# Weights packed in reading order, a transposed copy of x, packed bias columns and a four-block first stream in a hybrid encoder layer

## The chip, the core and the metric

The kernel runs on one core of a Trainium2 chip. The metric is device time in microseconds, the median of three runs: 1731.29 us before the change (1729.61 to 1732.01). The names of the engines are those of the profile: PE multiplies matrices (PEld is its weight load), DVE, ACT and POOL work elementwise, SP issues the DMAs.

## The reference

One layer of a hybrid encoder, for 256 tokens of 2048 channels, in float32:

```
proj   = x @ w_in + b_in                      # [256, 15384]
y_a    = forgetting_attention(q, k, v, log_sigmoid(f))          # 8 heads of 128
y_b    = u * (masked w_s @ group_layer_norm(v) + b_s)           # spatial gating, 8 groups
y_c    = gated_delta_rule(silu(conv4(qkv)), decays, betas)      # 8 heads, chunks
merged = sum_i sigmoid(gate_i) * (y_i @ w_proj_i)               # 3 x [1024, 2048]
x1     = layer_norm(2**0.25 * x + merged @ w_out)
h      = conv3(x1 @ w_up) + conv_b                              # [2048, 11008]
out    = layer_norm(2**0.25 * x1 + (silu(h_gate) * h_val) @ w_down)   # [5504, 2048]
```

The weights are 80 million float32 numbers and are each used once.

## The kernel before

Every large product is a **weight stream**. The helper `wload` (L117 to L125) brings 512 KB of weights into one of four `raw` buffers with one DMA on SP's queue (L122), and `split` (L113 to L115) makes two float32r parts of it: ACT copies the high part into `wh` (L114), DVE subtracts to get the low part `wl` (L115). There are four `wh` and four `wl` buffers. The activations are split in the same way, so a product is a sum of high by high, low by high and high by low.

`stream_b` (L162 to L184) computes two blocks of 128 channels for all 256 tokens: for each of 16 blocks of 128 input channels and for each of its two output blocks there is one matmul with 512 columns (L178: the high weights by x's high and low parts side by side) and one with 256 columns (L179: the low weights by the high part). In the text such two matmuls are called a pair; a stream has 32 pairs, and four 512 KB tiles feed it. `stream_a` (L127 to L160) computes 512 channels for the two token blocks with three matmuls of 512 columns each (L134 to L136).

The DeltaNet projections come first, as twelve streams of the kind `stream_b` (L814 to L840): four of keys, four of queries, four of values. Within the first, `load_x` (L249 to L254) loads x with the tokens on the partitions, transposes it on PE (L243) and splits it into `xhl`. After each stream comes an epilogue with a causal conv (L826 to L834), most of it on DVE. The projections of attention and spatial gating, the gates, the three branch projections, `w_out`, and the feed-forward part follow.

The smaller work of the mixers is written as Python generators in a list `queue`. After each of the 16 blocks of a stream `tick` runs the oldest generator to its next `yield`, so that this work lies between matmuls of the stream. `small_columns` (the gates' 24 columns, L280 to L377) and `gdn_decays` enter the list after the first stream, `gdn_keys` after the four key streams. `gdn_keys` multiplies key products into the decays `am` (DVE, L432), scales `am` (POOL, L443, by the factors `fa` of L439), sends its diagonal blocks through DRAM (L451, L454), inverts them by an elimination of 31 steps on POOL (L462, L464) and writes the result `td` (L467). `gdn_inverse`, put into the list after the last value stream, reads it into `T` (L482), transposes it on DVE (L488) and goes on on PE (L502).

A scheduler with a timeline model orders the instructions of each engine at build time; on the chip each engine follows its list strictly in order. SP too: a DMA that waits holds up every DMA behind it.

Columns of biases and conv weights are loaded as rows of 128 and transposed on PE by `rows_to_cols` (L224 to L232; the transpose is L229), ten uses' worth of columns in eight transposes. The mixing matrices of the spatial gating are transposed on PE as well (L775).

Of the kernel before, what the change touches and what calls it, by code (L numbers as in the profile page):

```python
# [10 lines left out]
F32 = mybir.dt.float32  # L11
# [8 lines left out]
P = 128  # L20
# [22 lines left out]

@with_exitstack
def trunk_kernel(ctx, tc, x, w_in, b_in, sgu_ln_g, sgu_ln_b, sgu_w, sgu_b, gdn_conv_w, gdn_a_log,
                 gdn_dt_bias, gdn_norm_g, w_proj_a, w_proj_b, w_proj_c, w_out, ln1_g, ln1_b,
                 ffn_w_up, ffn_conv_w, ffn_conv_b, ffn_w_down, ln2_g, ln2_b, out):
    nc = tc.nc
    x, w_in, sgu_w, gdn_conv_w = x[0], w_in[0], sgu_w[0], gdn_conv_w[0]
    w_proj = [w_proj_a[0], w_proj_b[0], w_proj_c[0]]  # L50
    w_out, ffn_w_up, ffn_conv_w, ffn_w_down = w_out[0], ffn_w_up[0], ffn_conv_w[0], ffn_w_down[0]
    out = out[0]

# [63 lines left out]
    def wload(src, k0, nk, c0, n, dst=None, low=nc.vector, ahead=150):  # L117
        """Weight rows k0*128.. (nk blocks), columns c0..c0+n: list over blocks of (high, low) views."""
        with tc.high_priority(offset=ahead):
            raw = wraw.tile([P, 1024], F32, tag="raw", name=nm("raw"))  # L120
            rv = raw[:, 0:nk * n].rearrange("p (k n) -> p k n", n=n)
# [6 lines left out]
    def stream_a(src, nkb, c0, lh, ll, k_off=0, tail=0, spare=(), spare_last=False, done=None, pre=None):  # L128
        """[tokens, 512] outputs for both token blocks; the last tail k blocks go block by block of tokens."""
# [9 lines left out]
        for k0 in range(0, head, 2):  # L139
            nk = min(2, head - k0)  # L140
            ws = wload(src, k_off + k0, nk, c0, 512)
# [8 lines left out]
        for i, k0 in enumerate(starts):  # L150
            j = i - (len(starts) - len(spare)) if spare_last else (i if i < len(spare) else -1)
            ws += wload(src, k_off + k0, min(2, nkb - k0), c0, 512, spare[j] if j >= 0 else None,
# [9 lines left out]
    def stream_b(src, c0, n, act, pre=None):  # L162
        """n//128 blocks of [128 channels, (main 256 | low part 256)]."""
        nb = n // P
        accs = [acc() for _ in range(nb)]
        nk = 1024 // n
        for k0 in range(0, KB, nk):
            if pre is not None:
                pre(k0)
            ws = wload(src, k0, nk, c0, n, ahead=150 if pre is None else 1)  # L170
            for j in range(nk):
                kb = k0 + j
                wh, wl = ws[j]
                for i in range(nb):
                    a = accs[i]
                    cs = slice(i * P, (i + 1) * P)
                    if kb < KB - 1:
                        nc.tensor.matmul(a, wh[:, cs], act[:, kb, :], start=kb == 0, stop=False)  # L178
                        nc.tensor.matmul(a[:, 0:S], wl[:, cs], act[:, kb, 0:S], start=False, stop=False)  # L179
                    else:  # L180
                        nc.tensor.matmul(a[:, 0:S], wl[:, cs], act[:, kb, 0:S], start=False, stop=False)  # L181
                        nc.tensor.matmul(a, wh[:, cs], act[:, kb, :], start=False, stop=True)  # L182
                tick()
        return accs  # L184

    def stream_b_halves(src, c0, act):
        """As stream_b for 2 blocks, the tokens block by block: [128 channels, (main 2 x 128 | low part 2 x 128)]."""
        accs = [acc() for _ in range(2)]
        ws = []
        for k0 in range(0, KB, 4):  # L190
            ws += wload(src, k0, 4, c0, 256, low=nc.gpsimd)
# [14 lines left out]
    def rsqrt(dst, src, n):  # L206
        """dst = src ** -0.5 for positive normal src, by Newton steps."""
# [7 lines left out]
    def rsqrt_column(dst, src):  # L215
        """The same for one column; the steps y <- y (y^2 src - 3) leave powers of two to the end."""
# [7 lines left out]
    def rows_to_cols(src_rows, nr, name):  # L224
        """DRAM rows [nr, 128] -> SBUF [128, nr]."""
        r = wk.tile([P, 512], F32, tag="wk", name=nm("rows"))
        nc.sync.dma_start(r[0:nr, 0:P], src_rows)
        p = mx()
        nc.tensor.transpose(p[:, 0:nr], r[0:nr, 0:P], ident[0:nr, 0:nr])  # L229
        c = const.tile([P, nr], F32, name=name)  # L230
        nc.vector.tensor_copy(c, p[:, 0:nr])
        return c  # L232

# [13 lines left out]
    x_sb = resp.tile([P, 2, D], F32, tag="res", name="x_sb")  # L247
# [76 lines left out]
        # softplus(z) = max(z, 0) + log1p(exp(-|z|)); z = -f for the forget gates, a + dt for the decays  # L324
# [12 lines left out]
        # log1p(e) = 2 atanh(e / (2 + e))  # L337
# [20 lines left out]
        # rows [16, 256] (forget: whole sequence; decay: per 128 tokens)  # L358
# [21 lines left out]
    def inv_norm(ss, name):  # L380
        """1 / norm [128 tokens, 2, 8] from sums of squares [128, 16]."""
# [750 lines left out]
```

## Time and profile before

| | us |
|---|---|
| median of three runs | 1731.29 |
| lowest and highest | 1729.61, 1732.01 |
| span of the profiled execution, first to last instruction | 1727.9 |
| PE busy | 1689.7 (98%) |
| DVE, ACT, POOL busy | 1119.2, 780.9, 262.5 |
| HBM read | 321.38 MB, 188 GB/s over the span |
| DMA engines, mean busy share | 63.0% for the queue of the program's DMAs |

The page gives the span of the profiled execution and no separate time for it; the median of the timed runs is 3.4 us above that span. PE is busy in nearly every slice of the span. What it leaves idle, some 38 us, lies in four places: the first ten microseconds, the stretch from 80 to 190 us, the first layer norm near 980 us, and the last layer norm after 1712 us.

### The profile page before, as it was taken

The page shows a single profiled execution, that of the slowest core. Times are in us where ns is not written, and L with a number is a line of the kernel's source. Part 1 is how long each engine was busy: PE and PEld are TensorE (multiplying, and loading weights), DVE is VectorE, ACT ScalarE, POOL GpSimd, SP SyncE. Part 2 cuts the span into 40 slices and gives each one's busy share as a digit, 9 for nine tenths or more (in the row PEclk, how much of TensorE's full clock was granted, in tenths as well). Part 3 has the DMA queues.
Part 4 walks back from the last instruction along what each step waited for, and adds up shares of the span by engine and source line. Part 5 has one row for each costly group of instructions (what it writes and reads, how often), then busy time and mean ns, then how long its engine had stood idle before and what let it go on. Part 6 is the DMA issues. An engine that isn't in the chain of part 4 may idle for free.

```text
span 1727.9 us, 22873 instructions
## 1 busy us (share of the span) xinstructions
PE 1689.7 (98%) x8738; PEld 1435.5 (83%) x8738; DVE 1119.2 (65%) x1516; ACT 780.9 (45%) x985; POOL 262.5 (15%) x213
## 2 busy tenths in 40 slices
PE   8989999999999999999999999999999999999996
PEld 7877898888888888888888788888888888888885
DVE  5999555577665555555555777775567776567767
ACT  5543444354444444444443355544344544344542
POOL 0259030304230000100100301110001110001102
PEclk9999899999999999999999999999999999999998
DMA  8563646766666666666676476666666665666653
GB/s 239 171 183 97 172 113 196 240 182 173 194 191 206 200 201 206 199 198 200 198 268 213 148 219 183 184 185 195 192 190 185 184 188 191 194 185 194 185 178 112
DMA packets 245249, 325.51 MB, mean 188 GB/s; under 512 B 18844, under 2 KB 159764, under 8 KB 244116
## 3 DMA queue, kind: packets, MB, share of 16 engines
q1 hardware_dynamic: 245140, 324.06, 63.0%
q8 instruction: 68, 1.11, 0.3%
q14 instruction: 41, 0.34, 0.1%
HBM read 321.38 MB, written 2.64 MB: 188 GB/s over the span
## 4 chain that ended last, share of the span: by engine, by line
PE 91%; DVE 6%; issue 1%; DMA 1%; ACT 0%; DVEq 0%; SPq 0%; ACTq 0%
PE acc L178 24%; PE acc L136 16%; PE acc L134 16%; PE acc L135 16%; PE acc L179 12%; PE acc L182 2%; DVE wl L115 1%; DVE cv L832 1%; PE acc L181 1%; DVE z L974 1%; PE mx L243 1%; DVE cv L830 0%; DVE z L973 0%; ACT wh L114 0%; DMA x_sb<-in_x_dram 0%
## 5 line engine op out<-in xcount | busy, mean ns | idle before, releaser
L115 DVE TENSOR_TENSOR wl<-raw,wh 128x1024 fp32r<-128x1024 f32 (+1 forms) x568 | 716.7, 1263 | 494.7 <-ACT wh L114 485.8
L114 ACT ACTIVATE wh<-raw 128x1024 fp32r<-128x1024 f32 x572 | 603.8, 1056 | 686.4 <-PE acc L136 417.2
L178 PE MATMUL acc<-x1hl,wh 128*128 128x512 f32 x1260 | 446.6, 398 | 0.0
L179 PE MATMUL acc<-x1hl,wl 128*128 128x256 f32 x1260 | 354.0, 281 | 0.0
L178 PEld LDWEIGHTS acc<-x1hl,wh 128*128 128x128 f32 x1260 | 236.7, 188 | 56.4
L178 PE MATMUL acc<-xhl,wh 128*128 128x512 f32 x720 | 259.6, 402 | 2.4 <-ACT wh L114 2.4
L179 PEld LDWEIGHTS acc<-x1hl,wl 128*128 128x128 f32 x1260 | 238.1, 189 | 1.7
L134 PE MATMUL acc<-wh,xhl 128*128 128x512 f32 x576 | 226.6, 393 | 0.0
L135 PE MATMUL acc<-wl,xhl 128*128 128x512 f32 x576 | 224.5, 390 | 0.0
L136 PE MATMUL acc<-wh,xhl 128*128 128x512 f32 x576 | 224.4, 390 | 0.0
L179 PE MATMUL acc<-xhl,wl 128*128 128x256 f32 x720 | 205.8, 286 | 7.2 <-DVE wl L115 7.2
L178 PEld LDWEIGHTS acc<-xhl,wh 128*128 128x128 f32 x720 | 137.0, 191 | 33.0 <-ACT wh L114 2.7
L1076 POOL TENSOR_TENSOR cvv<-cvv,cvg 128x256 f32<-128x256 f32 x43 | 56.5, 1332 | 607.3 <-DVE cvv L1047 607.3
L179 PEld LDWEIGHTS acc<-xhl,wl 128*128 128x128 f32 x720 | 137.9, 192 | 11.8 <-DVE wl L115 10.5
L136 PE MATMUL acc<-wh,aL 128*128 128x512 f32 x328 | 127.6, 389 | 0.0
L135 PE MATMUL acc<-wl,aH 128*128 128x512 f32 x328 | 127.6, 389 | 0.0
L134 PE MATMUL acc<-wh,aH 128*128 128x512 f32 x328 | 127.6, 389 | 0.0
L136 PEld LDWEIGHTS acc<-wh,xhl 128*128 128x128 f32 x576 | 108.1, 188 | 22.5
L135 PEld LDWEIGHTS acc<-wl,xhl 128*128 128x128 f32 x576 | 108.2, 188 | 21.9
L134 PEld LDWEIGHTS acc<-wh,xhl 128*128 128x128 f32 x576 | 108.2, 188 | 21.9
L945 POOL TENSOR_TENSOR merged<-merged,wk 128x512 f32<-128x512 f32 x16 | 28.3, 1787 | 362.9 <-DVE wk L943 362.9
L135 PEld LDWEIGHTS acc<-wl,aH 128*128 128x128 f32 x328 | 61.6, 188 | 12.9
(352 smaller groups left out, 1898.3 us busy)
## 6 DMA issues: line engine op xcount, KB each, us to landing
raw<-in_w_in_dram SPq DMA_DIRECT2D x240, 512.0 KB, 3.7
raw<-in_ffn_w_up_dram SPq DMA_DIRECT2D x172, 512.0 KB, 3.9
raw<-in_ffn_w_down_dram SPq DMA_DIRECT2D x84, 512.0 KB, 4.3
raw<-in_w_out_dram SPq DMA_DIRECT2D x32, 512.0 KB, 4.4
raw<-in_w_proj_a_dram SPq DMA_DIRECT2D x16, 512.0 KB, 3.6
raw<-in_w_proj_b_dram SPq DMA_DIRECT2D x16, 512.0 KB, 3.6
raw<-in_w_proj_c_dram SPq DMA_DIRECT2D x16, 512.0 KB, 3.7
wk<-in_b_in_dram SPq DMA_DIRECT2D x18, 256.0 KB, 3.9
```

The source lines that it names most:

```text
L114: nc.scalar.activation(dst_h, src, AF.Copy)
L115: low.tensor_sub(dst_l, src, dst_h.bitcast(F32))
L134: nc.tensor.matmul(a, lh(kb, tb), w[0], start=kb == 0, stop=False)
L135: nc.tensor.matmul(a, lh(kb, tb), w[1], start=False, stop=False)
L136: nc.tensor.matmul(a, ll(kb, tb), w[0], start=False, stop=kb == nkb - 1)
L178: nc.tensor.matmul(a, wh[:, cs], act[:, kb, :], start=kb == 0, stop=False)
L179: nc.tensor.matmul(a[:, 0:S], wl[:, cs], act[:, kb, 0:S], start=False, stop=False)
L181: nc.tensor.matmul(a[:, 0:S], wl[:, cs], act[:, kb, 0:S], start=False, stop=False)
L182: nc.tensor.matmul(a, wh[:, cs], act[:, kb, :], start=False, stop=True)
L243: nc.tensor.transpose(pv[:, i, tb * P:(tb + 1) * P], src(kb, tb), ident)
L945: nc.gpsimd.tensor_add(merged[:, tb, cs], merged[:, tb, cs], gts[tb])
L1076: nc.gpsimd.tensor_mul(cv, cv, cvg[i])
```

## The change

All arrays are now prepared on the host before the launch in the order in which the kernel reads them, and the kernel reads them by new addresses. The part of the diff that does this on the host is not shown in full; its core is `pack`, which lays each 256- or 512-column piece of a weight matrix out as [128 partitions, blocks of 128 rows, columns]. A 512 KB tile is then 4 KB in one run on each partition, where it was four runs of 1 KB or two of 2 KB.

```
+    def tiles(src, nkb, n, first=0):
+        def at(t, k0, nk):
+            return bass.AP(tensor=src.tensor, offset=src.offset + first + t * nkb * P * n + k0 * n,
+                           ap=[[nkb * n, P], [1, nk * n]])
+        return at
...
-            nc.sync.dma_start(rv, src[k0 * P:(k0 + nk) * P, c0:c0 + n].rearrange("(k p) n -> p k n", p=P))
+            nc.sync.dma_start(raw[:, 0:nk * n], src(k0, nk))
...
-    def stream_b(src, c0, n, act, pre=None):
+    def stream_b(srcs, n, act, steps=None, pre=None, more=()):
...
-        accs = [acc() for _ in range(nb)]
+        accs = list(more) + [acc() for _ in range(nb * len(srcs) - len(more))]
...
+        for nk in steps or [nk] * (KB // nk):
...
+            ws = [wload(src, k0, nk, n, ahead=150 if pre is None else 1) for src in srcs]
...
-    def load_x(kb):
-        for tb in range(2):
-            nc.sync.dma_start(x_sb[:, tb, kb * P:(kb + 4) * P], x[tb * P:(tb + 1) * P, kb * P:(kb + 4) * P])
-        for k in (kb, kb + 2):
-            transpose_split(xhl[:, k:k + 2, 0:S], xhl[:, k:k + 2, S:2 * S],
-                            lambda kk, tb: x_sb[:, tb, kk * P:(kk + 1) * P], [k, k + 1])
+    def load_x(k0, nk):
+        nc.sync.dma_start(x_sb[:, k0 * S:(k0 + nk) * S], bass.AP(tensor=x_t.tensor, offset=x_t.offset + k0 * S,
+                                                                 ap=[[KB * S, P], [1, nk * S]]))
+        split(xhl[:, k0:k0 + nk, 0:S], xhl[:, k0:k0 + nk, S:2 * S], x_sv[:, k0:k0 + nk])
...
-        wsn = slot("wsn").rearrange("p (g s) -> p g s", s=P)
-        nc.sync.dma_start(wsn[:, 0:8, :], sgu_w.rearrange("g t s -> t g s"))
...
+        nc.sync.dma_start(wsn[:, 0:W], sgu_wt)
...
-        for q in range(2):
-            p4 = heads4(mx())
-            for i in range(4):
-                nc.tensor.transpose(p4[:, i, :], wsn[:, q * 4 + i, :], ident)
-            nc.scalar.activation(g.wsT[:, q * 4:q * 4 + 4, :], p4, AF.Copy)
...
+    def load_first(k0, nk):
+        load_x(k0, nk)
+        if k0 == 2:
+            nc.sync.dma_start(cmix, cols[:, 0:C_MIX])
+
+    for n, jps in enumerate(((4, 5), (6,), (7,), (0,), (1,), (2,), (3,), (8,), (9,), (10,), (11,))):
...
+            accs = stream_b([tile_of(t_ch, T_QKV + jp) for jp in jps], 256, xhl, steps=(1, 1, 2, 4, 4, 4),
+                            pre=load_first, more=[mx(), mx()])
             queue += [small_columns(), gdn_decays()]
...
-        if n == 3:
+        if n == 2:
             queue.append(gdn_keys())
...
-    fcw = [rows_to_cols(ffn_conv_w[t].rearrange("(j p) -> j p", p=P), 2 * NF, f"fcw{t}") for t in range(3)]
-    fcb = rows_to_cols(ffn_conv_b[0].rearrange("(j p) -> j p", p=P), 2 * NF, "fcb")
+    nc.sync.dma_start(cffn, cols[:, C_FW:C_ALL])
```

The first two key streams are now one stream of four blocks of output channels; its loads come in steps of 1, 1, 2, 4, 4 and 4 blocks of input channels, two weight tiles and one piece of x for each step. The other ten DeltaNet streams are as before. `rows_to_cols` is gone: its columns come in two DMAs (`cmix`, `cffn`). The matmuls of the streams are L192 and L193 in the changed file, the splits L127 and L128, the weight DMAs L134, x's DMAs L256.

On PE the program begins, before, with transposes of x (`mx` and `acc` are buffers of PSUM, `wh` and `wl` the two parts of a weight tile):

```order
L243 MATMUL mx_116<-ident,x_sb 128x128
L243 MATMUL mx_123<-ident,x_sb 128x128
L243 MATMUL mx_116<-ident,x_sb 128x128 x3
L243 MATMUL mx_123<-ident,x_sb 128x128 x3
L243 MATMUL mx_154<-ident,x_sb 128x128
L243 MATMUL mx_161<-ident,x_sb 128x128
L178 MATMUL acc_112<-xhl,wh_132 128x512
L178 MATMUL acc_113<-xhl,wh_132 128x512
```

and now with four matmuls on the first block of input channels:

```order
L192 MATMUL mx_113<-xhl,wh_122 128x512
L192 MATMUL mx_114<-xhl,wh_122 128x512
L192 MATMUL acc_115<-xhl,wh_128 128x512
L192 MATMUL acc_116<-xhl,wh_128 128x512
L193 MATMUL mx_113<-xhl,wl_123 128x256
L193 MATMUL mx_114<-xhl,wl_123 128x256
L193 MATMUL acc_115<-xhl,wl_129 128x256
L193 MATMUL acc_116<-xhl,wl_129 128x256
```

The 32 transposes are gone, and four accumulators are open instead of two.

On SP's queue the write of the elimination's result, `td`, stands before the change behind the 48th weight tile, the last of the DeltaNet streams:

```order
L122 DMA raw_47_1754<-in_w_in_dram 128x4x256
L122 DMA raw_48_1776<-in_w_in_dram 128x4x256
L467 DMA td_843<-ab_1_848 64x1024
L122 DMA raw_49_1827<-in_w_in_dram 128x4x256
L122 DMA raw_50_1874<-in_w_in_dram 128x4x256
```

and now behind the 54th, with the read of `T` five weight tiles further on:

```order
L134 DMA raw_53_1784<-in_w_ch_dram 128x1024
L134 DMA raw_54_1831<-in_w_ch_dram 128x1024
L467 DMA td_806<-ab_1_811 64x1024
L134 DMA raw_55_1871<-in_w_ch_dram 128x1024
L134 DMA raw_56_1893<-in_w_ch_dram 128x1024
L134 DMA raw_57_1967<-in_w_ch_dram 128x1024
L134 DMA raw_58_2040<-in_w_ch_dram 128x1024
L134 DMA raw_59_2100<-in_w_ch_dram 128x1024
L482 DMA T_1_1861<-td_806 32x16x32 x4
```

The first wide stream takes 12 DMAs for what were 8 tiles, so the 54th is the 50th of before: `td` has moved two tiles later in the weights, and `T`, which stood behind the 57th, two tiles earlier.

On DVE, the factors `fa` for the scaling of `am` came before the change after the products with `am` (L432), between parts of the conv and weight splits:

```order
L432 TENSOR_TENSOR am_1_486<-mx_17_786,am_1_486 128x512
L432 TENSOR_TENSOR am_1_486<-mx_18_799,am_1_486 128x512
L211 TENSOR_TENSOR sm_1_820<-rk_819 128x16
L828 TENSOR_TENSOR up0_105<-acc_11_988,wk_11_1078 128x256
L212 SCALAR_TENSOR_TENSOR sm_1_820<-sm_1_820,ssk_759 128x16
L828 TENSOR_TENSOR up1_106<-acc_12_989,wk_12_1087 128x256
L213 SCALAR_TENSOR_TENSOR rk_819<-sm_1_820,rk_819 128x16
L437 TENSOR_TENSOR fv_831<-beta_379,rk_819 128x16
L439 TENSOR_TENSOR fa_833<-fv_831,rk_819 128x16
```

and now come before them:

```order
L437 TENSOR_TENSOR fv_794<-beta_450,rk_782 128x16
L439 TENSOR_TENSOR fa_796<-fv_794,rk_782 128x16
L441 TENSOR_TENSOR fw_623<-fw_623,fa_796 128x8
L128 TENSOR_TENSOR wl_34_1194<-raw_34_1191,wh_34_1193 128x1024
L432 TENSOR_TENSOR am_1_557<-mx_7_723,am_1_557 128x512
L432 TENSOR_TENSOR am_1_557<-mx_8_736,am_1_557 128x512
L128 TENSOR_TENSOR wl_35_1216<-raw_35_1213,wh_35_1215 128x1024
L432 TENSOR_TENSOR am_1_557<-mx_9_749,am_1_557 128x512
L432 TENSOR_TENSOR am_1_557<-mx_10_762,am_1_557 128x512
```

From the sums of squares (L382) to the last of `fa` and L432 there were 30 instructions on DVE, and there are 21 now.

## Rows read from the trace of the kernel before

**Rows 1.** The page: busy time, share of the span and instructions of each engine.
```profile
PE 1689.7 (98%) x8738; PEld 1435.5 (83%) x8738; DVE 1119.2 (65%) x1516; ACT 780.9 (45%) x985; POOL 262.5 (15%) x213
```

**Rows 2.** Stretches: length, busy us (instructions) of each engine, granted clock, DMA share, GB/s.
```profile
0.00:10.00 10.00, 4.81 (x19) 3.60 (x19) 2.65 (x6) 3.84 (x5) 1.64 (x14) 1.00 0.79 241
...
4.00:8.00 4.00, 2.81 (x11) 1.90 (x12) 0.89 (x2) 1.77 (x3) 0.00 (x0) 1.00 1.02 351
...
80.00:170.00 90.00, 81.44 (x470) 69.18 (x469) 89.62 (x130) 41.31 (x58) 67.17 (x74) 1.00 0.47 129
...
175.50:179.70 4.20, 3.41 (x10) 2.71 (x11) 3.90 (x5) 3.60 (x7) 0.00 (x0) 0.59 1.02 315
```

**Rows 3.** Waits from 75 to 200 us: PE's, SP's: us in total, times, longest.
```profile
PE acc L179 <- DVE wl L115: 7.2, 8, 2.4
...
SPq L467 <- POOL ab L464: 10.5, 1, 10.5
```

**Rows 4.** Timeline, PE: start, us, line, operation, count [idle before, releaser].
```profile
4.34 0.66 PE L243 MATMUL mx<-ident,x_sb 128*128 128x128 f32 x2 [4.34 <-DMA x_sb<-in_x_dram]
...
7.82 1.22 PE L178 MATMUL acc<-xhl,wh 128*128 128x512 f32 x2
...
13.51 1.03 PE L243 MATMUL mx<-ident,x_sb 128*128 128x128 f32 x8
...
15.08 0.39 PE L178 MATMUL acc<-xhl,wh 128*128 128x512 f32 x1
...
15.42 0.40 PE L178 MATMUL acc<-xhl,wh 128*128 128x512 f32 x1
...
26.38 2.94 PE L305 MATMUL mx<-xhl,wst 128*48 128x512 f32 x12
...
39.11 0.39 PE L182 MATMUL acc<-xhl,wh 128*128 128x512 f32 x1
```

**Rows 5.** Timeline, POOL: decays, scaling, first and last step of the elimination.
```profile
75.66 3.75 POOL L399 TENSOR_TENSOR am<-cnat,gbc 128x1024 f32<-128x1024 f32 x2 [73.30 <-DVE ssk L433]
...
89.23 1.44 POOL L456 TENSOR_SCALAR_AFFINE_SELECT ab<-ab 64x1024 f32<-64x1024 f32 x1
100.31 5.66 POOL L443 TENSOR_TENSOR am<-am,fa 128x1024 f32<-128x1024 f32 x2 [9.64 <-DVE fa L439]
114.45 1.34 POOL L462 TENSOR_TENSOR gw<-ab 64x31 f32<-64x31 f32 x1 [8.48 <-DMA ab<-ad]
...
169.07 0.33 POOL L464 TENSOR_TENSOR ab<-ab,gw 64x31 f32<-64x31 f32 x1
```

**Rows 6.** Timeline, PE and DVE: the cumulative sums' matmuls, products with am, factors fa.
```profile
65.56 0.39 PE L360 MATMUL mx<-utri,glog 128*16 128x128 f32 x2
...
97.55 1.27 DVE L432 TENSOR_TENSOR am<-mx,am 128x512 f32<-128x512 f32 x2
...
99.99 0.18 DVE L439 TENSOR_TENSOR fa<-fv,rk 128x16 f32<-128x16 f32 x1
```

**Rows 7.** Timeline, SP, DVE and PE, from the elimination's result to its use.
```profile
169.43 0.47 SPq L467 DMA_DIRECT2D td<-ab  x1
...
172.78 0.39 PE L182 MATMUL acc<-xhl,wh 128*128 128x512 f32 x1
175.53 0.50 PE L178 MATMUL acc<-xhl,wh 128*128 128x512 f32 x1 [2.36 <-ACT wh L114]
...
185.67 3.01 SPq L482 DMA_DIRECT2D T<-td  x4
...
193.10 2.50 DVE L488 STREAM_TRANSPOSE M<-T 128x512 f32<-128x512 f32 x4 [0.66 <-DMA T<-td]
...
196.51 2.85 PE L502 MATMUL mx<-M,am 128*96 128x64 f32 x32
```

**Rows 8.** The page's DMA issues: issuer, count, KB each, median us to landing.
```profile
raw<-in_w_in_dram SPq DMA_DIRECT2D x240, 512.0 KB, 3.7
...
raw<-in_w_out_dram SPq DMA_DIRECT2D x32, 512.0 KB, 4.4
```

More of the change, by code (lines that the diff above doesn't have):

```diff
@@ L854, in bias_tile, with proj_nat @@
         return b
-    def proj_nat(dst, off):
+    def proj_nat(dst, off, t):
         for c in range(2):
             b = bias_tile(off + c * 512)
-            accs = stream_a(w_in, KB, off + c * 512, xh, xl)
+            accs = stream_a(tile_of(t_tok, t + c), KB, xh, xl)
             for tb in range(2):
@@ L868, in trunk_kernel @@
     for jp in range(8):
-        accs = stream_b(w_in, O_FQ + jp * 256, 256, xhl)
+        accs = stream_b([tile_of(t_ch, T_FQK + jp)], 256, xhl)
         for i in range(2):
@@ L891, in trunk_kernel @@
         b = bias_tile(O_GG + c * 512)
-        accs = stream_a(w_in, KB, O_GG + c * 512, xh, xl)
+        accs = stream_a(tile_of(t_tok, T_GG + c), KB, xh, xl)
         for tb in range(2):
@@ L1015, in trunk_kernel @@
                 spare += zip(pieces(slot("sh", F32R), 2), pieces(slot("sl", F32R), 2))
-        stream_a(w_out, KB, c * 512,
+        stream_a(tile_of(tiles(w_out, KB, 512), c), KB,
                  lambda kb, tb: mH[kb // 8][:, kb % 8, tb * P:(tb + 1) * P],
@@ L1026, in trunk_kernel, with up_tile @@
     cf = ctx.enter_context(tc.tile_pool(name="cf", bufs=3))
-    fcw = [rows_to_cols(ffn_conv_w[t].rearrange("(j p) -> j p", p=P), 2 * NF, f"fcw{t}") for t in range(3)]
-    fcb = rows_to_cols(ffn_conv_b[0].rearrange("(j p) -> j p", p=P), 2 * NF, "fcb")
+    cffn = fp.tile([P, 8 * NF], F32, name="cffn")
+    nc.sync.dma_start(cffn, cols[:, C_FW:C_ALL])
+    fcw = [cffn[:, t * 2 * NF:(t + 1) * 2 * NF] for t in range(3)]
+    fcb = cffn[:, 6 * NF:8 * NF]
+    NU = NF // 2
+    def up_tile(half, blk, n):
+        first = half * D * DFF
+        if n == 2:
+            return tile_of(tiles(w_up, KB, 256, first), blk // 2)
+        return tile_of(tiles(w_up, KB, 128, first + NU * D * 256), 0)
     l2g = fp.tile([P, D], F32, name="l2g")
@@ L1103, in trunk_kernel, with _packed, pack, columns @@
                      tail=nb if last else 0, spare=spare, done=residual2)
-_INS = ["x", "w_in", "b_in", "sgu_ln_g", "sgu_ln_b", "sgu_w", "sgu_b", "gdn_conv_w", "gdn_a_log", "gdn_dt_bias",
-        "gdn_norm_g", "w_proj_a", "w_proj_b", "w_proj_c", "w_out", "ln1_g", "ln1_b", "ffn_w_up", "ffn_conv_w",
-        "ffn_conv_b", "ffn_w_down", "ln2_g", "ln2_b"]
+_INS = ["x", "x_t", "w_ch", "w_tok", "w_small", "cols", "b_in", "sgu_ln_g", "sgu_ln_b", "sgu_wt", "sgu_b", "gdn_a_log",
+        "gdn_dt_bias", "gdn_norm_g", "w_proj", "w_out", "ln1_g", "ln1_b", "w_up", "w_down", "ln2_g", "ln2_b"]
 _OUTS = [((1, S, D), "float32")]
+def _packed(inputs):
+    import numpy as np
+    v = {k: np.asarray(a) for k, a in inputs.items()}
+    def pack(w, n):
+        k, m = w.shape
+        return w.reshape(k // P, P, m // n, n).transpose(2, 1, 0, 3).ravel()
+    def columns(a):
+        return a.reshape(-1, P).T
+    w, b = v["w_in"][0], v["b_in"][0]
+    bs = np.zeros((P, 1), np.float32)
+    bs[0:8, 0] = b[O_FF:O_FF + 8]
+    bs[8:24, 0] = b[O_GA:O_GA + 16]
+    v["x_t"] = v["x"][0].T.reshape(KB, P, S).transpose(1, 0, 2).reshape(P, KB * S)
+    v["w_ch"] = np.concatenate([pack(w[:, o:o + n], 256) for o, n in ((O_G, 3 * W), (O_FQ, 2 * W), (O_SU, W))])
+    v["w_tok"] = np.concatenate([pack(w[:, o:o + n], 512)
+                                 for o, n in ((O_FV, W), (O_SV, W), (O_GG, W), (O_GT, 3 * D))])
+    small = np.concatenate([w[:, O_FF:O_FF + 8], w[:, O_GA:O_GA + 16]], axis=1)
+    v["w_small"] = small.reshape(KB, P, 24).transpose(1, 0, 2).reshape(P, KB * 24)
+    v["cols"] = np.concatenate([columns(b[O_G:O_G + 3 * W]), columns(v["gdn_conv_w"][0]), columns(b[O_FQ:O_FQ + 2 * W]),
+                                columns(b[O_SU:O_SU + W]), bs, columns(v["ffn_conv_w"][0]),
+                                columns(v["ffn_conv_b"][0])], axis=1)
+    v["sgu_wt"] = v["sgu_w"][0].transpose(2, 0, 1).reshape(P, W)
+    v["w_proj"] = np.concatenate([pack(v[f"w_proj_{i}"][0], 512) for i in "abc"])
+    v["w_out"] = pack(v["w_out"][0], 512)
+    up = v["ffn_w_up"][0]
+    v["w_up"] = np.concatenate([pack(up[:, o:o + m], n) for h in range(2)
+                                for o, m, n in ((h * DFF, DFF - P, 256), (h * DFF + DFF - P, P, P))])
+    v["w_down"] = pack(v["ffn_w_down"][0], 512)
+    return {n: v[n] for n in _INS}
 def kernel(**inputs):
@@ L1117 @@
     from concourse.bass_utils import run_bass_kernel_spmd as _run
+    inputs = _packed(inputs)
     nc = _bacc.Bacc("TRN2", target_bir_lowering=False, num_devices=1)
```

119 lines of the change are left out of this document (55 added, 64 removed).

## The prediction

> **What bounds the kernel now.** I read the busy shares first: PE is busy for 1689.7 of the span's 1727.9 us [rows 1]. So the steady streams can give nothing except PE work taken away; the change can win only where PE idles or where it removes PE instructions. The second view was the table of stretches, to find the idle time. In the first 10 us PE is busy for 4.81, and from 80 to 170 for 81.44 of 90 [rows 2]. The third was the list of waits from 75 to 200: the longest single wait there, 10.5 us, is SP's own, for the end of POOL's elimination [rows 3]. The timeline, read last, joins these. At the start PE has transposes only, from 4.34, and its first weight matmul comes at 7.82 [rows 4]. Near 170 SP's `td` is held for POOL until 169.43, the weight loads behind it on SP's queue are held too, and PE runs dry: 384 pairs (twelve streams of 32) are done at 172.78 + 0.39 = 173.2, the next matmul is at 175.53 [rows 7].
>
> A pair of matmuls takes 0.34 us between rounded starts (15.08 to 15.42) [rows 4]; I use 0.345, and 11.0 us for a stream of 32.
>
> **Part 1, the start.** Before, two streams (64 pairs) and the 16 matmuls of the gates' columns end at 39.11 + 0.39 = 39.5 [rows 4]. After, there are no transposes and PE begins with weight matmuls. It then needs the first piece of x and its split, where it needed x alone (4.34): I take 4.7. From there 64 pairs are 22.1 us. A start at the low clock costs something: after the pause near 175 the granted clock is 0.59 in a stretch of 4.2 us, which is the 1.2 GHz level for most of it, and ten matmuls are busy for 3.41 us [rows 2] where five pairs take 1.7; I charge 1.7. The gates' matmuls take 2.94 us for 12, so 3.9 for 16 [rows 4], and some 0.3 for their sums.
>
> The loads might not keep up. Six MB of weights and x must arrive in about 22 us, or 270 to 290 GB/s, through four `raw` buffers, and from 4 to 8 us the DMA engines are already full (share 1.02) and move 351 GB/s [rows 2]. So supply just exceeds demand. I take 0.5 us of waits; 0 if 351 holds throughout, 2.8 if the small first steps bring it down to 300. Sum: 4.7 + 22.1 + 1.7 + 0.5 + 3.9 + 0.3 = 33.2, a gain of 6.3 (4 to 7).
>
> **Part 2, the gates' chain begins later.** `small_columns` enters the list after the first stream, and that stream is now twice as long. The matmuls of the cumulative sums (L360) had 138 pairs ahead of them and now have 170, by the order of PE. They were at 65.56 [rows 6]; 32 more pairs cost 11.0 and the start gives 6.3 back, so they move to 70.3, 4.7 later. All that POOL does with the decays moves with them: it was done at 89.23 + 1.44 = 90.67 [rows 5] and will be at 95.4.
>
> Then POOL waited 9.64 us for `fa` before the scaling at 100.31 [rows 5]. On DVE `fa` (99.99) stood behind the products with `am` (97.55), among weight splits and conv work [rows 6]; in the new order `fa` stands before L432. From the sums of squares to this point DVE has 21 instructions for 30. So two edits oppose each other: the head of the chain is 4.7 later, and the wait at its middle can shrink. Scaling cannot begin before POOL's 95.4; if the 9.64 stay whole it begins at 105.0. I take 96, near the lower end, since the DVE order removes exactly the instructions that `fa` stood behind. From the start of the scaling to the end of the elimination it was 169.07 + 0.33 - 100.31 = 69.1 us [rows 5]. With the same length it ends at E = 165.1, against 169.4.
>
> The 69.1 is not a constant: POOL's first elimination step on a 64x31 tile took 1.34 us, and its last instruction, on such a tile too, 0.33 [rows 5], while DVE was busy for 89.62 of the 90 us around them [rows 2]. The Trainium skill, "SBUF — State Buffer", section "SBUF: two separate sides", states that a DVE instruction with two inputs in SBUF and a GpSimd instruction that reads SBUF take the same pair of ports, exclusively, for a whole instruction. The trace agrees as far as these two durations go, and by that rule the elimination's length would follow what DVE does beside it. DVE's load there falls by nothing in the new order, so I keep 69.1, and allow 5 us to either side. With the ends for the scaling this makes E 160 to 174, and 179 if both ends fall the wrong way.
>
> **Part 3, from the elimination to its use.** Before, SP issued `td` at 169.43, `T` at 185.67, and the matmuls that use it (L502) ran at 196.51 [rows 7]. Now `td` stands two tiles later in the weights and `T` five tiles behind it instead of nine. Two tiles are 16 pairs, 5.5 us, so the queue gives PE some more work before `td` can stop it. When `td` is held until E, the loads behind it resume then; the first of them gives PE its matmul 175.53 - 169.43 = 6.1 us later. `T` waits until raw buffers come free for the tiles between, about two tiles' time after E: I take E + 8. From the issue of `T` to L502 was 196.51 - 185.67 = 10.8 us, for the read, DVE's transposes and POOL's writes [rows 7]. So L502 cannot start before E + 18.8 = 183.9.
>
> PE would arrive there sooner. 384 pairs were done at 173.2, now 166.9; then L502 had 426 pairs ahead of it and now has 412, so 28 follow (9.7 us). In the old stretch from 175.53 to 196.51, the 42 pairs explain 14.5 of 21.0 us; 1.7 of the rest is the low clock and some 0.9 a wait for bias rows that goes, which leaves up to 3.9 for other matmuls. PE arrives at about 180 and waits 4 us. This is the new late thing: a wait at L502, in place of the wait for weights near 173. Compared at equal work: before, with 14 pairs fewer, L502 would have stood at 196.51 - 4.8 = 191.7; now it stands at 183.9, a gain of 7.8. A pause of 4 us should lower the clock again, as the 2.36 did [rows 7, 2]; I take off 1.5. Net 6.3. Part 1's gain is inside this figure and is not added again: what the chain gives decides how much of it survives.
>
> **Part 4, what is removed later.** One transpose of a bias row, eight of the mixing matrices and four of FFN columns go from PE: eight transposes take 1.03 us with pipelined ends [rows 4], so 13 take at most 1.7; I take 1.4 (0 to 1.7). The two DMAs of columns come long before their use and lie beside full PE work. The new addresses turn 1 or 2 KB runs into 4 KB; in the steady stages PE is busy throughout and the DMA engines are at 63%, so a faster DMA shows nowhere, and a slower one neither until it has slowed by 1/0.63 = 1.59.
>
> **Sum.** 6.3 + 1.4 = 7.7 us. The profiled span 1727.9 becomes 1720.2; the median of the runs lay 3.4 above that span, so 1723.6.
>
> **Rivals.**
> (a) The elimination ends early enough that PE never waits at L502. The DVE order speaks for it, the later head of the chain against. L502 is reached at 180 when E is 161 or less; the gain is then 191.7 - 180 = 11.7, + 1.4 = 13.1: about 1718.2.
> (b) Slower: the chain moves by all of its 4.7 us, because `fa` comes no sooner beside conv work on a full DVE, and the elimination runs up to 5 us longer. Scaling at 105.0 gives E = 174.1, L502 at 192.9: 1.2 lost, 1.5 for the clock, 1.4 back: 1.3 slower. With 5 us more it is 6.3 slower, 1737.6. It decides from E = 172.8. For it: POOL's 9.64 us wait and the 10.5 us that SP waited show that this chain was late already. Against: the order of DVE.
> (c) The first stream starves: 512 KB buffers filled by quarter and half tiles, at a DMA share of 1.02. If part 1 gains 1 instead of 6.3, L360 moves 10 later, POOL is ready at 100.7, E is 170 and L502 at 188.8: gain 2.9 - 1.5 + 1.4 = 2.8: about 1728.5.
> (d) The changed layout slows all weight DMAs. `w_out`, whose rows stand 8,192 bytes apart, takes 4.4 us for a tile, `w_in`, at 61,536, takes 3.7 [rows 8]: a factor of 1.19, which is hidden below 1.59; a factor of 2 would make DMA the bound at 2 x 0.63 = 1.26 times the span, about 2180 us. The Trainium skill, "DMA: Bandwidth & Descriptors", section "Latency and other measured facts", states that row pitches at large powers of two lower the rate of HBM, up to a half at several MiB. The new pitches, 16 and 32 KB, are powers of two but far below those; no run here shows more than the 1.19.
>
> **How the numbers follow.** Forecast (gain 4 to 11.5) 0.54; (a) 0.21; (b) 0.13; (c) 0.10; (d) 0.02. This kernel's three runs lie within 0.14%, and 0.2%, 3.5 us, is what can be told from no change. Faster by more than that: the forecast, (a), and a third of (c), 0.54 + 0.21 + 0.04, so 0.79. Within: most of (b) and the rest of (c), 0.13. Slower: the long end of (b), and (d), 0.08. The range reaches from just under (a) to the point where (b) begins: 1716 to 1731; its lower end is E at 160 and PE's arrival 2 us sooner.
>
> **What would show it.** Right: no transposes of x; first weight matmul near 4.7; two streams and the gates' matmuls done near 33; L360 near 70; scaling near 96 with almost no wait; `td` near 165; L502 near 184 behind a pause of a few us; streams later on at 0.345 a pair. Wrong: weight waits of more than 3 us before 33 (c); scaling near 105 (b); no pause before L502 (a); raw tiles that take over 5 us and PE waiting for DMAs after 200 (d). A gain or loss behind 200 us beyond 1.7 us would mean that I have missed a mechanism.

## The result and the profile after

The changed kernel takes 1739.38 us (median of 4 runs, 1738.52 to 1744.06), against 1730.45 for the kernel before on the same chip (4 runs): 1.0061 of its time, 95% interval 1.0047 to 1.0076. Slower, where 1723.6 was forecast, and outside the range of 1716 to 1731.

The page's first part, which answers to [rows 1]:

```profile
PE 1697.2 (98%) x8690; PEld 1435.8 (83%) x8690; DVE 1120.2 (65%) x1509; ACT 781.9 (45%) x985; POOL 259.8 (15%) x213
```

PE has 48 instructions fewer, and is busy 7.5 us longer, of a span that is 8.8 longer (1736.7 us). So most of the loss is not idle time. To find it I counted the 512-column stream matmuls of both timelines (5832 in each) and compared when the same one starts (numbers from 0):

| number | before, us | after, us | after less before |
|---|---|---|---|
| 128 | 61.9 | 58.7 | -3.25 |
| 376 | 170.2 | 169.9 | -0.38 |
| 384 | 175.5 | 172.6 | -2.89 |
| 512 | 254.2 | 256.9 | +2.79 |
| 1408 | 509.6 | 511.4 | +1.76 |
| 3520 | 1025.5 | 1026.7 | +1.21 |
| 4480 | 1316.0 | 1320.1 | +4.13 |
| 5376 | 1583.8 | 1590.9 | +7.04 |
| 5824 | 1709.7 | 1718.3 | +8.63 |

Two losses are to be seen: some 6 us between 60 and 250 us, and 7.4 us in three steps behind 1170 us. The first is 2.9 us up to 170 and 5.7 us behind 173; in between, 2.5 come back, because the pause of before near 173 is gone. The second loss I look at first. The three steps are the three groups of `w_down`, and within each the difference grows evenly, by 0.48 us for 64 matmuls: 14.51 us before, 14.99 after. The groups of instructions by line, of before and of after (busy us, mean ns of one):

```profile
L134 PE MATMUL acc<-wh,aH 128*128 128x512 f32 x328 | 127.6, 389 | 0.0
```

```profile
L146 PE MATMUL acc<-wh,aH 128*128 128x512 f32 x328 | 130.0, 396 | 0.0
```

and one stretch of the first group, before and after (columns as in [rows 2]):

```profile
1186.00:1246.00 60.00, 60.00 (x266) 49.67 (x266) 30.55 (x28) 23.34 (x22) 0.00 (x0) 1.00 0.63 196
```

```profile
1186.00:1246.00 60.00, 60.00 (x257) 48.24 (x257) 30.08 (x28) 22.43 (x22) 0.00 (x0) 1.00 0.59 189
```

PE is busy throughout in both, at the full clock of 2.4 GHz, and does 257 matmuls instead of 266. `stream_a` with the same shapes in the token-major projections keeps its 14.51 us for 64. What differs is the place of the operands in SBUF. In the program's allocations `aH` began at 151136 bytes and `wh` at 40544, a distance of 110592, 27 x 4096. Now the four conv columns are no longer in the pool of constants, so `wh` is at 39136, and `cffn` stands at the head of the FFN's pool, so `aH` is at 151104: a distance of 27 x 4096 + 1376. In the other streams the distance between the two buffers is a multiple of 4096 in both kernels.

The first loss, by stretches of after:

```profile
80.00:170.00 90.00, 81.44 (x465) 69.80 (x465) 89.03 (x127) 42.91 (x61) 65.66 (x70) 0.96 0.42 141
...
98.00:106.00 8.00, 5.97 (x26) 5.18 (x27) 7.69 (x18) 3.86 (x6) 2.35 (x2) 0.79 0.38 132
116.00:124.00 8.00, 6.64 (x28) 5.61 (x29) 8.00 (x20) 1.96 (x5) 2.95 (x8) 0.79 0.58 185
...
180.00:188.00 8.00, 5.97 (x28) 5.26 (x29) 8.00 (x17) 4.38 (x7) 0.00 (x0) 0.79 0.76 220
200.00:220.00 20.00, 20.00 (x137) 17.18 (x136) 4.27 (x6) 5.54 (x8) 0.00 (x0) 0.66 0.09 34
```

and of before, where the clock was low too:

```profile
172.00:180.00 8.00, 4.89 (x20) 3.74 (x19) 4.20 (x5) 4.95 (x8) 0.91 (x1) 0.79 1.04 326
...
200.00:220.00 20.00, 20.00 (x176) 18.27 (x175) 5.21 (x10) 5.42 (x9) 0.00 (x0) 0.83 0.25 69
```

From 80 to 170 PE is busy for the same 81.44 us as in [rows 2]; its idle time has neither shrunk nor grown, but the granted clock is 0.96 where it was 1.00. Summed over 60 to 240 us, stretch length times (1 - clock) is 11.9 us after and 5.1 before: 6.8 us of clock lost, which bounds what it cost, since PE is idle in part of these stretches. Half of that lies in the two stretches near 100 and 120; the other half is the stretch from 200 to 220: 20 x (0.83 - 0.66) = 3.4. There PE works on the inverse. Its order reads so, the first block before, the second after:

```profile
202.42 2.85 PE L511 MATMUL mx<-P,T 96*96 96x64 f32 x32
205.21 2.16 PE L520 MATMUL mx<-T,P 32*64 32x32 f32 x32
207.30 3.67 PE L528 MATMUL mx<-M,am 64*64 64x64 f32 x32
...
211.28 0.63 PE L178 MATMUL acc<-xhl,wh 128*128 128x512 f32 x1
...
213.84 0.40 PE L178 MATMUL acc<-xhl,wh 128*128 128x512 f32 x1
214.16 2.07 PE L537 MATMUL mx<-gw,T 64*64 64x64 f32 x32
```

```profile
190.68 1.49 PE L502 MATMUL mx<-M,am 128*96 128x64 f32 x16
...
196.49 2.85 PE L511 MATMUL mx<-P,T 96*96 96x64 f32 x32
199.27 2.05 PE L520 MATMUL mx<-T,P 32*64 32x32 f32 x32
...
201.91 1.14 PE L528 MATMUL mx<-M,am 64*64 64x64 f32 x16
...
204.56 1.97 PE L528 MATMUL mx<-M,am 64*64 64x64 f32 x16
...
208.04 1.97 PE L537 MATMUL mx<-gw,T 64*64 64x64 f32 x16
...
211.51 1.97 PE L537 MATMUL mx<-gw,T 64*64 64x64 f32 x16
```

Before, L528 was one group of 32 and five pairs followed it, during which the clock came back (a 512-column matmul goes from 0.63 to 0.40 us). After, the four halves of L528 and L537 have only two pairs between one and the next, and all of it, to 216 us, lies in the low clock (a 512-column matmul still takes 0.63 us at 214.21), though PE is never idle there.

### The profile page after: what moved, and what is told of

Its sections match the earlier page's. It is cut to its first block, busy times and chain, and to the rows that moved or that the text cites. A ratio compares the mean times of both kernels' runs of the same rounds, so it can differ in the third digit from the quotient of the medians.

```text
span 1736.7 us, 22777 instructions
## 1 busy us (share of the span) xinstructions
PE 1697.2 (98%) x8690; PEld 1435.8 (83%) x8690; DVE 1120.2 (65%) x1509; ACT 781.9 (45%) x985; POOL 259.8 (15%) x213
## 3 DMA queue, kind: packets, MB, share of 16 engines
q1 hardware_dynamic: 95856, 324.06, 57.3%
## 4 chain that ended last, share of the span: by engine, by line
PE 92%; DVE 6%; DMA 1%; issue 1%; ACT 1%; DVEq 0%; SPq 0%; ACTq 0%
PE acc L192 24%; PE acc L148 16%; PE acc L146 16%; PE acc L147 16%; PE acc L193 12%; PE acc L196 2%; DVE wl L128 1%; PE acc L195 1%; DVE z L979 1%; DVE cv L839 1%; DMA raw<-in_w_ch_dram 1%; DVE sm L226 0%; ACT wh L127 0%; DVE z L978 0%; PE mx L248 0%
## 5 line engine op out<-in xcount | busy, mean ns | idle before, releaser
L128 DVE TENSOR_TENSOR wl<-raw,wh 128x1024 fp32r<-128x1024 f32 (+1 forms) x572 | 716.5, 1254 | 498.1 <-ACT wh L127 497.3
L127 ACT ACTIVATE wh<-raw 128x1024 fp32r<-128x1024 f32 (+1 forms) x576 | 604.6, 1050 | 678.5 <-PE acc L148 422.9
L192 PE MATMUL acc<-x1hl,wh 128*128 128x512 f32 x1260 | 446.5, 398 | 0.0
L193 PE MATMUL acc<-x1hl,wl 128*128 128x256 f32 x1260 | 354.0, 281 | 0.0
L192 PEld LDWEIGHTS acc<-x1hl,wh 128*128 128x128 f32 x1260 | 236.7, 188 | 56.3
L192 PE MATMUL acc<-xhl,wh 128*128 128x512 f32 x690 | 253.8, 408 | 2.8 <-ACT wh L127 1.7
L193 PEld LDWEIGHTS acc<-x1hl,wl 128*128 128x128 f32 x1260 | 238.1, 189 | 1.7
L193 PE MATMUL acc<-xhl,wl 128*128 128x256 f32 x690 | 197.7, 288 | 4.6 <-DVE wl L128 4.4
L192 PEld LDWEIGHTS acc<-xhl,wh 128*128 128x128 f32 x690 | 133.4, 194 | 33.5 <-ACT wh L127 2.1
L193 PEld LDWEIGHTS acc<-xhl,wl 128*128 128x128 f32 x690 | 133.8, 194 | 8.2 <-DVE wl L128 6.8
L148 PEld LDWEIGHTS acc<-wh,aL 128*128 128x128 f32 x328 | 61.8, 188 | 15.1
```

Of the source, the lines that this page charges most:

```text
L127: nc.scalar.activation(dst_h, src, AF.Copy)
L128: low.tensor_sub(dst_l, src, dst_h.bitcast(F32))
L148: nc.tensor.matmul(a, ll(kb, tb), w[0], start=False, stop=kb == nkb - 1)
```

## The experiments

All ratios are set against the kernel before, run on the same chip with the kernel in question. Not all kernels ran on the same chip; where two that did not are compared, the ratios count more than the medians.

**Address modulo 64.** `cffn` is allocated eight columns wider.

```
-    cffn = fp.tile([P, 8 * NF], F32, name="cffn")
+    cffn = fp.tile([P, 8 * NF + 8], F32, name="cffn")
```

> The changed kernel with eight unused columns (32 bytes) behind the FFN columns cffn, so that aH and aL begin at the addresses modulo 64 bytes that they had before the change (32, as wh and wl), and nothing else moves. Theory A (place in SBUF): the three w_down stages run 64 matmuls in 14.5 us again instead of 15.0, the time falls by about 7.4 us, to some 1.0007 of the kernel before (1732). Rival B (the packed w_down or its DMAs slow the matmuls): 15.0 us stay, the time stays at 1.006 (1739 to 1740).

1740.04 us, ratio 1.0042 (1.0027 to 1.0058). In the trace `w_down` takes 14.87, 14.87 and 14.94 us for 64 in its groups. Theory A in this form is wrong: the residue modulo 64 was restored and the pace was not. The median is where B had it, but B is not supported by the pace, since 14.87 is not 15.0 and the packing was the same.

**The kernel before, with `aH` moved.** `l2b` is eight columns wider; the distance is 27 x 4096 + 32.

```
-    l2b = fp.tile([P, D], F32, name="l2b")
+    l2b = fp.tile([P, D + 8], F32, name="l2b")[:, 0:D]
```

> The kernel before with eight unused columns behind l2b, so that aH and aL begin at 0 modulo 64 bytes while wh and wl stay at 32. Theory A: the w_down stages, and no other, go from 14.5 to 15.0 us for 64 matmuls; about 1738 to 1739, 1.004 of before. Rival B: no difference, 1731.

1736.61 us, 1.0028 (1.0014 to 1.0042). The groups by line:

```profile
L134 PE MATMUL acc<-wh,aH 128*128 128x512 f32 x328 | 129.7, 396 | 0.0
```

14.93 us for 64, in `w_down` alone. The old layout of the weights slows as well: B falls, although the time rose by less than A's 7 us.

**All operands moved.**

```
-    ones = const.tile([P, P], F32, name="ones")
+    ones = const.tile([P, P + 8], F32, name="ones")[:, 0:P]
```

> The kernel before with eight unused columns behind the constant ones, so that every buffer that a stream's matmul reads (wh, wl, xhl, aH, aL) begins at 0 modulo 64 bytes instead of 32. Theory A1 (what counts is that the two operands of a matmul lie differently): no difference, 1731. Theory A2 (a stationary operand that begins at 0 is slow whatever the other does): every stage slows by 3.4%, some 1785.

1730.85 us, 0.9996 (0.9984 to 1.0008), each stage at its old pace. What counts is where the two operands lie to each other: A1, not A2.

**The weights on one side, all activations on the other.**

```
+    pad = hl.tile([P, 8], F32, tag="pad", name="pad")
+    nc.gpsimd.memset(pad, 0.0)
     xhl = hl.tile([P, KB, 2 * S], F32R, tag="hl", name="xhl")
```

> The kernel before with 32 bytes between the weight buffers and all that is allocated behind them: wh and wl stay at 32 modulo 64 bytes; xhl, x1hl, the split branch results and aH, aL go to 0. Theory A1 (operands that lie differently): every stream slows by 3.4%, the ones with weights stationary too, some 1785. Theory A2 (stationary at 0 is slow): only the streams with activations stationary slow (w_proj, w_out, w_down and the token-major projections, about 740 of the 1728 us), some 1756, and the FFN's up streams stay at their pace. Rival B (no effect of place): 1731.

1743.73 us, 1.0065 (1.0046 to 1.0084); neither 1785 nor 1756. Every `stream_a` slowed as A1 says (14.93 for 64), but the streams with weights stationary became faster, the up streams among them: 22.23 us for 64 pairs instead of 22.60. Their groups (before had 446.6 and 398):

```profile
L178 PE MATMUL acc<-x1hl,wh 128*128 128x512 f32 x1260 | 439.3, 391 | 0.0
```

So distance 0 is the best yet seen where activations are stationary, and not the best where weights are. That was not expected by any of the theories.

**The old distance in the changed kernel.** `cffn` goes to the pool of constants.

```
-    cffn = fp.tile([P, 8 * NF], F32, name="cffn")
+    cffn = const.tile([P, 8 * NF], F32, name="cffn")
```

> The changed kernel with the FFN columns cffn allocated in the pool of constants instead of the FFN's pool. That restores the distance from wh to aH (27 times 4096 bytes, as before the change; it was 32 bytes short of 27 times 4096 plus 1408 after it). Theory C (a stream's pace depends on the distance between its two operands, by more than 64 bytes): the w_down stages run 64 matmuls in 14.5 us, and some 7.4 us go; 1731 to 1733. Rival B (the packed w_down itself is slow): 15.0 us stay, 1739.

1733.22 us, 1.0015 (1.0003 to 1.0026). The stretch of the first `w_down` group again:

```profile
1186.00:1246.00 60.00, 60.00 (x266) 49.70 (x265) 30.61 (x29) 23.41 (x23) 0.00 (x0) 1.00 0.64 194
```

266 matmuls, as before the change, with the packed weights. C holds. Of the loss of 9 us the distance is 6.2 by the medians, 7.2 by the spans of the two traces (1736.7 and 1729.5) and 8.0 by the ratios.

**Two narrow streams first.** On top of that:

```
-    for n, jps in enumerate(((4, 5), (6,), (7,), (0,), ...
+    for n, jps in enumerate(((4,), (5,), (6,), (7,), (0,), ...
...
-                            pre=load_first, more=[mx(), mx()])
+                            pre=load_first)
```

> As the kernel with the restored distance, but the first two key streams are two streams of two blocks again; packing, transposed x and packed columns stay. Theory W (the wide stream delays the gates' chain by 32 pairs, and the low clock near 210 us follows from it): decays on POOL begin near 73 instead of 83.8, the elimination ends before 168 instead of 173, and the time is 4 to 7 us below the kernel with the wide stream, about 1725 to 1728. Rival P (the wide stream costs nothing; the start with packed data does): no difference, 1731 to 1733.

1733.22 us, 1.0010 (0.9999 to 1.0021): no difference. The decays begin at 77.26 and the elimination ends at 169.6, both earlier than with the wide stream, though not as early as W had them (73 and 168); but the start gains less (1.1 us at matmul 128 instead of 3.25), and from 200 to 220 the clock is lower still:

```profile
200.00:220.00 20.00, 20.00 (x121) 17.04 (x120) 2.63 (x4) 4.11 (x7) 0.00 (x0) 0.52 0.11 37
```

W had a shorter stretch of low clock follow from an earlier elimination; here it is longer, in the slowest of the 12 runs, and over all 12 the granted clock of the whole kernel is 0.987, for 0.986 with the wide stream. With no gain in time, W falls, and the order on PE, which this kernel shares with the wide one, was to be tested.

**The small matmuls grouped** (on the wide stream with the old distance).

```
             nc.scalar.activation(p2[0:64], p8[0:64], AF.Copy)
             p2s.append(p2)
+        for _ in range(3):
             yield
...
+        for _ in range(5):
             yield
...
-            yield
+        yield
+        yield
```

> As the kernel with the restored distance, with one more edit: in the inverse the two halves of L528, of L537 and of L589 follow each other without a yield between, and three, five and two yields stand behind them, so that PE has 9 pairs between these groups of small matmuls as it had before the change, where it now has two pairs between halves. Theory K (the low clock from 203 to 216 us comes from small matmuls with few stream matmuls between them): the stretch of granted clock 0.5 near 210 is about 6 us long, as before, instead of 13, and the time falls by about 3 us, from 1733 to about 1730. Rival L (the low clock follows from when the elimination ends, not from the order on PE): no difference in the stretch or the time.

1728.40 us, 0.9991 (0.9978 to 1.0003), 0.24% or 4.2 us below the same kernel ungrouped, by the ratios (4.8 by the medians). The stretch of low clock near 210 is some 10 us, not the 6 that K expected and not 13. The same stretch ungrouped, then grouped:

```profile
200.00:220.00 20.00, 20.00 (x140) 17.14 (x139) 4.28 (x6) 5.54 (x8) 0.00 (x0) 0.66 0.12 40
```

```profile
200.00:220.00 20.00, 20.00 (x163) 17.98 (x163) 4.88 (x8) 4.48 (x6) 0.00 (x0) 0.74 0.15 53
```

PE does 163 matmuls there instead of 140. K is supported in sign and size of the time; L is not. The two profiled executions alone do not show the gain: their spans are 1729.8 grouped and 1729.5 ungrouped, since this one had longer low stretches near 120 and 186. The grouped one is among the slowest of its 11 runs, the ungrouped one the fastest of its 12. The granted clock of all runs shows it: the mean is 0.989 grouped and 0.986 ungrouped, and 0.003 of 1730 us is 5 us, an estimate that takes all lost clock for lost time.

**Both:** narrow streams and grouping.

> The narrow first streams (two streams of two blocks, packed weights, transposed x, restored distance) with the small matmuls of the inverse grouped as in the run before. Theory K: the low clock near 210, 20 us long with the narrow streams, becomes some 6 to 10 us long, and the time falls by 3 to 5 us below 1733, to about 1729, so that the wide stream is worth nothing either way. Rival W (the narrow start is better by the earlier elimination, and only the low clock hid it): 1726 or less.

1729.10 us, 0.9984 (0.9975 to 0.9992), 0.26% or 4.5 us below the narrow ungrouped kernel, by the ratios (4.1 by the medians). The mean granted clock is 0.990 over the 12 runs, for 0.987. From 200 to 220 the clock is 0.79 and PE does 138 matmuls instead of 121 (from 198 to 222 the clock is 0.79 for 0.57):

```profile
200.00:220.00 20.00, 20.00 (x138) 17.62 (x139) 5.67 (x7) 7.21 (x11) 0.00 (x0) 0.79 0.16 53
```

K for the second time. The wide and the narrow stream come out alike, grouped and ungrouped.

**A scan of distances.** The first try moved the weight buffers apart, so that the distance changed from tile to tile.

```
-            hh, ll = dst or (wspl.tile([P, 1024], F32R, tag="wh", name=nm("wh")), ...
+            d = 8 * (place[0] % 4)
+            hh, ll = dst or [wspl.tile([P, 1056], F32R, tag=t, name=nm(t))[:, d:d + 1024] for t in ("wh", "wl")]
```

> The kernel before with 128 bytes between the weight buffers, and each stream's wh and wl beginning 0, 32, 64 or 96 bytes into them, in turn; five work buffers instead of six, to make room. So the distance between the two operands of a stream's matmuls takes all 16 values modulo 512 bytes, in steps of 32, tile by tile. Theory C: the time of a tile's matmuls follows that distance; in w_down the fastest at distance 0, some 3% above it at 32, at 352 and at 384; in the up streams it is about 1.7% below that of distance 0 at 480. Rival B: all tiles of a stage take the same.

1744.84 us, one run. It didn't separate the distances: `w_down` took 14.83 to 14.87 in all groups and the up streams 22.41. A tile's dozen matmuls lie between tiles of other distances, and show no pace of their own. The next two kept one distance for a whole stage:

```
+        o = (0, 16, 32)[gi]
+        aH = actp.tile([P, 16 * S + 128], F32R, tag="aH", name=nm("aH"))[:, o:o + 16 * S].rearrange(...)
```

> The kernel before with 64 bytes between the weight buffers and all behind them, and aH and aL of the three groups of w_down placed so that their distance to wh modulo 512 bytes is 64, 128 and 192. Theory C: each group has a steady pace of its own, at or above the 14.5 us for 64 matmuls of distance 0, and the up streams and the token-major streams leave their old pace of 45.2 us for 128 pairs and 14.5 us. Rival B: all stay at the paces of the kernel before.

> The same with 128 bytes behind the weight buffers, and distances of 256, 320 and 384 for the three groups of w_down. Theory C: paces of their own for each, the last group near 14.85 us for 64, as the kernel with eight more columns had at 384. Rival B: all as in the kernel before.

1747.22 and 1744.91 us, one run each. `w_down`, 64 matmuls, and the up streams, 64 pairs, over all kernels that kept one distance:

| stationary less moving, modulo 512 bytes | `w_down`, us | up streams, us |
|---|---|---|
| 0 | 14.51 | 22.60 |
| 32 | 14.93 | |
| 64, 128, 192 | 14.93, 14.93, 14.65 | |
| 256 | 14.51 | |
| 320, 352, 384 | 14.94, 15.00, 14.87 | |
| 384 (-128) | | 22.46 |
| 448 (-64) | | 22.36 |
| 480 (-32) | | 22.23 |

For `w_down` 0 and 256 are alike, and nothing tried was faster. The value at 192 is from the last group alone, of 11 blocks. The distance modulo 512 is not all of it: at 384, in the kernel with eight more columns, the last group took 14.94 where the first two took 14.87, and at 128 the projections of the third scan took 14.87 where `w_down` took 14.93 in the second.

**Both distances chosen.** The grouped kernel with `x1hl` 32 bytes up in a buffer that is 256 bytes longer.

```
-    x1hl = hl.tile([P, KB, 2 * S], F32R, tag="hl", name="x1hl")
+    x1hl = hl.tile([P, KB * 2 * S + 64], F32R, tag="hl", name="x1hl")[:, 8:8 + KB * 2 * S].rearrange(...)
```

> The wide stream, restored distance and grouped small matmuls, with x1hl moved up by 32 bytes and everything behind it by 256 bytes, so that the up streams have the distance -32 (where another kernel showed 22.23 us for 64 pairs) and w_down a distance that is a multiple of 256. Theory C: up streams at 22.23 us for 64 pairs instead of 22.60, over 1260 pairs 7.3 us less; w_down at 14.51; the time 1721 to 1722, below both kernels by more than 0.4%. Rival B (the pace in that other kernel came from something else that moved there): 1728.

1722.79 us, 0.9940 (0.9925 to 0.9955), for the 1721 to 1722 that C expected: below both kernels. Up streams 22.23, `w_down` 14.51. The groups by line:

```profile
L192 PE MATMUL acc<-x1hl,wh 128*128 128x512 f32 x1260 | 439.3, 391 | 0.0
...
L146 PE MATMUL acc<-wh,aH 128*128 128x512 f32 x328 | 127.6, 389 | 0.0
```

Between the traces of the grouped kernel and of this one the three up stages give 2.7, 3.0 and 2.0 us, 7.6 together, for the 7.3 expected; the medians, of two chips, differ by 5.6, the ratios by 0.51%.

## Why the prediction was wrong

The step that failed first is its opening: "the steady streams can give nothing except PE work taken away". A busy share of 100% at full clock was read as a fixed pace. The pace depended on where the operands lay, and the change moved them without saying so: an edit priced at nothing (columns in one tile, in another pool) cost 7.4 us in the trace, and with the distance put back the changed kernel ran at 1.0015 of before instead of 1.0061. No rival had it. The prediction's last sentence, that more than 1.7 us behind 200 us would mean a missed mechanism, caught it.

Part 1, the start: a term mis-sized. Forecast 6.3 us, measured 3.25 at matmul 128, below its lower end of 4. PE began even earlier than taken:

```profile
3.97 1.19 PE L192 MATMUL mx<-xhl,wh 128*128 128x512 f32 x2 [3.97 <-ACT wh L127]
4.96 1.05 PE L192 MATMUL acc<-xhl,wh 128*128 128x512 f32 x2
...
11.15 0.72 PE L192 MATMUL acc<-xhl,wh 128*128 128x512 f32 x2 [1.65 <-ACT wh L127]
...
14.37 0.73 PE L192 MATMUL mx<-xhl,wh 128*128 128x512 f32 x2 [0.63 <-ACT wh L127]
15.62 0.50 PE L193 MATMUL mx<-xhl,wl 128*128 128x256 f32 x2 [0.53 <-DVE wl L128]
```

Two 512-column matmuls start 0.85 us before the next kind (4.96 to 5.81), 0.42 each, which is the pace of the 1.2 GHz level, and this lasts to 8.4 us; the granted clock of the stretch from 4 to 8 reads 1.00, so it rests on the pace alone. The three waits for splits of late loads sum to 2.8 us, the upper end that the text gave; 0.5 was taken. The 64 pairs end at 32.3 instead of 29.0: 3.97 to begin, 22.6 for 64 pairs at the full pace (22.1 was taken, from rounded starts), 2.2 for the slow pace (1.7 was taken) and 2.8 of waits make 31.6 of it. Before, transposes of x stood in part of the slow stretch: six took 1.54 us from 5.29, where eight took 1.03 from 13.51.

Part 2: the chain of the gates. The decays moved by 8.1 us, not 4.7, 3 of them from part 1:

```profile
83.75 3.75 POOL L399 TENSOR_TENSOR am<-cnat,gbc 128x1024 f32<-128x1024 f32 x2 [81.39 <-DVE ssk L433]
...
104.24 5.58 POOL L443 TENSOR_TENSOR am<-am,fa 128x1024 f32<-128x1024 f32 x2 [5.64 <-DVE am L432]
...
172.73 0.33 POOL L464 TENSOR_TENSOR ab<-ab,gw 64x31 f32<-64x31 f32 x1
```

The scaling came at 104.24, not 96. `fa` did come sooner after the head of the chain (17.8 us, for 24.5 before), as the order of DVE promised, but not as soon as POOL: it was ready at 101.53, 2.9 us behind POOL's 98.60, and the scaling then waited 2.7 us more for the products with `am` that had changed places with it. So I looked at one input of the instruction and forgot the other. And counting DVE's instructions was not enough: on the way to `fa` one on 16 columns (L226) took 5.07 us from 92.34 and ended as POOL's selection on `dt` did, at 97.4, where the same took 0.17 us at 99.90, with POOL idle. The prediction let DVE delay POOL and not POOL delay DVE; no run tests this. From the scaling on the length was right: 68.8 us to the end at 173.06, for 69.1. Rival (b), whose condition was an end behind 172.8, was the case that came, with 0.13. By its own sum this end costs 0.3 us; with the distance put back, 2.6 us were measured (1.0015).

Part 3: the use came 17.6 us after the elimination, at 190.68, for 18.8; the step held, and with this end it leaves 1 us of gain instead of 7.8. The wait expected at L502 stood elsewhere:

```profile
182.03 0.75 PE L475 MATMUL mx<-ident,kT 128*128 128x128 f32 x4 [3.85 <-DVE vn L574]
```

The clock was priced once, 1.5 us for one pause; up to 6.8 more were lost to it than before, half of that without a pause, through an order of small matmuls on PE that stood in the new program to be read, and was not read behind L502. All runs show how large this term is. With the distance put back, the mean granted clock is 0.986 over 12 runs, for 0.991 over the 23 runs of the kernel before on the same chip. That is some 7 to 8 us, while the time is only 2.6 longer; so the rest of the change did win some 4 to 6 us, and the clock took them back. (An estimate: 7 by the 1.45 us for 0.001 of clock that the 23 runs show among themselves, 8 if all lost clock is lost time.)

Part 4 held: from matmul 512 to 3520 the difference falls by 1.6 us, for 1.4. Rival (d) did not come: the same bytes took less of the DMA engines, 57.3% of the span for the 63.0 of before, in 95,856 packets for 245,140, and PE's time in the steady stages shows nothing of it either way:

```profile
q1 hardware_dynamic: 95856, 324.06, 57.3%
```

The rule of the Trainium skill on row pitches ("DMA: Bandwidth & Descriptors", section "Latency and other measured facts") is for pitches far larger, which no run here has. At 16 KB, 32 KB and the 86 KB of `w_down`, which the prediction left out, tiles land in 3.4 to 4.5 us in the median, for 3.6 to 4.4 before: nothing that PE's time shows behind the first stream.

So the loss of about 9 us is some 6 to 8 from the distance and some 4 from the order of the small matmuls (4.2 and 4.5 in two pairs of kernels); with both put back, the rest of the change is left with 0.9991 of before (0.9978 to 1.0003), no difference that can be told. The prediction also took the noise from three runs within 0.14%; the 23 runs of the kernel before on one chip spread over 0.5%. Why the earlier elimination of the narrow streams brings nothing, and how much of the first low stretches, near 100 and 118 us, belongs to the wide stream, was not separated.

## What to carry to other kernels

Before an edit is costed at nothing, compare the allocations: what moves in memory can change the pace of an engine that is busy all the time, and a count of the same instruction in both timelines shows it where busy shares don't. When two inputs of a waiting instruction swap places, follow both. Short matmuls spread thinly through a stream can hold the low clock longer than the same matmuls in groups with more of the stream between them (0.986 and 0.987 of the clock over all runs here, for 0.989 and 0.990); read the order on the bounding engine, to the end of the region, for where they stand. And where one profile of each kernel doesn't show a gain that the times show, look at the granted clock of every run.

## What the runs showed that was not expected

The pace of a full stream of matmuls depends on the distance of its two operands in SBUF: with activations stationary 14.51 us for 64 matmuls at 0 and 256 bytes (modulo 512), 14.65 to 15.00 at all others tried, and with weights stationary 22.60 for 64 pairs at 0 but 22.23 at -32. Moving both by 32 bytes changes nothing (0.9996). Only the effect is shown; its cause in the hardware is not, nor whether it repeats every 256 or 512 bytes.
